# Batch normalization over 512 MiB on one core: one DMA ring in groups of three, or a load ring and a store ring with hand-placed semaphores

## The chip, the cores and the metric

The kernel runs on one core of one Trainium2 chip. The metric is the device time of one execution in microseconds (us). The kernel before was run nine times: its median is 2487.23 us, with the runs between 2486.8 and 2489.03 us.

## The reference

The reference is batch normalization in its inference form, on a float32 tensor of 32 x 256 x 128 x 128. Each of the 256 channels has its own four numbers (gamma, beta, running mean and running variance), so that the whole computation is one multiplication and one addition for each element:

```python
def reference(x, gamma, beta, running_mean, running_var):
    eps = 1e-5
    ...
    return gamma * (x - mean) / np.sqrt(var + eps) + beta
```

The input has 536.87 MB and the output has as much. Every byte is read once and written once.

## The kernel before

**Tiles.** The 256 channels are two blocks of 128, one channel in each of the 128 partitions of the on-chip memory. With 32 images this makes 64 tiles. A tile has 128 partitions x 16384 float32 elements, which is 8.389 MB; each partition's row of 64 KiB is contiguous in device memory, and so is the whole tile. There are three buffers (NBUF = 3) of that size, and a tile is changed in place.

**Parameters.** At the start ScalarE's queue issues four loads of 1 KB, one for each parameter vector (line 58). VectorE transposes them (line 66) and copies them into place (line 71), ScalarE takes the square root (line 78), and four short VectorE instructions (lines 85 to 88) make a scale and a shift for each channel.

**The main loop.** Tile i goes through three steps: load(i) (line 51) is one DMA from device memory into a buffer, compute(i) (line 93) is one VectorE instruction that multiplies by the scale and adds the shift, and store(i) (line 104) is one DMA from the buffer to device memory. Loads and stores are all issued by SyncE (SP in the profile), and so lie in one ring, which the profile calls q1. The order is written out by hand: GROUPS lists twenty groups of three tiles and two of two, and AHEAD is 0. For each group the kernel issues the computes, then the group's stores, then the loads of the next group. On SP's ring this gives three loads, three stores, three loads, three stores, and so on. The pool of three buffers puts in the waits: a load waits until the store that last used its buffer has landed, and a store waits for its compute. Such a wait stands on SP, and everything issued later by SP stands behind it. Where an instruction has to wait for more than one semaphore, a separate semaphore instruction of 17 ns is put ahead of it (42 ahead of stores, 22 ahead of loads).

Of the kernel before, what the change touches and what calls it, by code (L numbers as in the profile page):

```python
# [1 line left out]

# [4 lines left out]


NBUF = 3
GROUPS = [3] * 20 + [2, 2]  # L10

AHEAD = 0


@with_exitstack
def kernel(
    ctx: ExitStack,
    tc: tile.TileContext,
    x: bass.AP,
    gamma: bass.AP,  # L20
    beta: bass.AP,
    running_mean: bass.AP,
    running_var: bass.AP,
    out: bass.AP,
):
    nc = tc.nc
    eps = 1e-5
    f32 = mybir.dt.float32

    N, C, H, W = x.shape  # L30
    P = nc.NUM_PARTITIONS
    assert C % P == 0
    NCB = C // P
    HW = H * W
    NT = N * NCB
    B = 32
    NQ = P // B
    assert sum(GROUPS) == NT and max(GROUPS) <= NBUF

    params = ctx.enter_context(tc.tile_pool(name="params", bufs=1))  # L40
    data = ctx.enter_context(tc.tile_pool(name="data", bufs=NBUF))

    xr = x.rearrange("n (cb p) h w -> (n cb) p (h w)", p=P)
    outr = out.rearrange("n (cb p) h w -> (n cb) p (h w)", p=P)

    ctx.enter_context(tc.manual_schedule())
    tiles = {}

    def load(i):
        t = data.tile([P, HW], f32, tag="t")  # L50
        nc.sync.dma_start(out=t[:], in_=xr[i])  # L51
        tiles[i] = t


    rows = params.tile([B, C], f32, tag="rows")
    nc.vector.memset(rows, 0.0)  # L56
    for r, ap in enumerate((running_var, gamma, beta, running_mean)):
        nc.scalar.dma_start(out=rows[r : r + 1, :], in_=ap.rearrange("(o c) -> o c", o=1))

    for i in range(AHEAD + GROUPS[0]):  # L60
        load(i)

    eps_t = params.tile([P, 1], f32, tag="eps")
    nc.vector.memset(eps_t, eps)  # L64
    turned = params.tile([B, C], f32, tag="turned")
    nc.vector.transpose(out=turned[:], in_=rows[:])  # L66

    par = params.tile([P, NCB, 4], f32, tag="par")
    blocks = turned.rearrange("p (cb q r) -> p cb q r", cb=NCB, q=NQ)
    for q in range(NQ):  # L70
        nc.vector.tensor_copy(out=par[q * B : (q + 1) * B], in_=blocks[:, :, q, 0:4])  # L71
    var_t, gamma_t, beta_t, mean_t = (par[:, :, r] for r in range(4))

    scale_t = params.tile([P, NCB], f32, tag="scale")
    shift_t = params.tile([P, NCB], f32, tag="shift")
    tmp_t = params.tile([P, NCB], f32, tag="tmp")

    nc.scalar.activation(  # L78
        out=tmp_t[:],
        in_=var_t,  # L80
        func=mybir.ActivationFunctionType.Sqrt,
        bias=eps_t[:],
        scale=1.0,
    )
    nc.vector.reciprocal(out=tmp_t[:], in_=tmp_t[:])  # L85
    nc.vector.tensor_mul(out=scale_t[:], in0=gamma_t, in1=tmp_t[:])  # L86
    nc.vector.tensor_mul(out=tmp_t[:], in0=mean_t, in1=scale_t[:])  # L87
    nc.vector.tensor_sub(out=shift_t[:], in0=beta_t, in1=tmp_t[:])  # L88

    def compute(i):  # L90
        t = tiles[i]
        cb = i % NCB
        nc.vector.tensor_scalar(  # L93
            out=t[:],
            in0=t[:],
            scalar1=scale_t[:, cb : cb + 1],
            scalar2=shift_t[:, cb : cb + 1],
            op0=mybir.AluOpType.mult,
            op1=mybir.AluOpType.add,
        )  # L100

    def store(i):
        t = tiles.pop(i)
        nc.sync.dma_start(out=outr[i], in_=t[:])  # L104


    first = 0
    for g, size in enumerate(GROUPS):
        idxs = range(first, first + size)
        for i in idxs:  # L110
            compute(i)
        for i in idxs:
            store(i)
        first += size
        more = GROUPS[g + 1] if g + 1 < len(GROUPS) else 0
        for i in range(first + AHEAD, min(first + AHEAD + more, NT)):
            load(i)


# [1 line left out]
_INS = ['x', 'gamma', 'beta', 'running_mean', 'running_var']  # L121
_OUTS = [((32, 256, 128, 128), 'float32')]


# [23 lines left out]
```

## Time and profile before

| | before |
|---|---|
| median of nine runs | 2487.23 us |
| the profiled execution, its whole time | 2488.09 us |
| span of the profiled execution | 2486.3 us |
| VectorE busy | 566.0 us (23% of the span) |
| ScalarE busy | 1.6 us |
| bytes moved by DMA | 1073.77 MB, a mean of 432 GB/s |
| one VectorE instruction on a tile | 8812 ns |
| one load, from issue to landing (median) | 58.0 us |
| one store, from issue to landing (median) | 49.1 us |

The profile's page gives the busy time of the engines, then the span in 40 equal slices with the busy share of the 16 DMA engines and the rate that they reached, then the DMA queues, the chain of work that ended last, and the groups of instructions. Line numbers such as L93 are lines of the kernel. A trailing q (SPq, ACTq) means an engine's queue of instructions, where DMAs are issued and where waits stand. The timeline lists instructions by their start. The "us to landing" of a DMA counts from its issue, so it holds the time in which the DMA stood behind others in its ring.

### The profile page before, as it was taken

The page shows a single profiled execution, that of the slowest core. Times are in us where ns is not written, and L with a number is a line of the kernel's source. Part 1 is how long each engine was busy: PE and PEld are TensorE (multiplying, and loading weights), DVE is VectorE, ACT ScalarE, POOL GpSimd, SP SyncE. Part 2 cuts the span into 40 slices and gives each one's busy share as a digit, 9 for nine tenths or more (in the row PEclk, how much of TensorE's full clock was granted, in tenths as well). Part 3 has the DMA queues.
Part 4 walks back from the last instruction along what each step waited for, and adds up shares of the span by engine and source line. Part 5 has one row for each costly group of instructions (what it writes and reads, how often), then busy time and mean ns, then how long its engine had stood idle before and what let it go on. Part 6 is the DMA issues. An engine that isn't in the chain of part 4 may idle for free.

```text
span 2486.3 us, 383 instructions
## 1 busy us (share of the span) xinstructions
DVE 566.0 (23%) x75; ACT 1.6 (0%) x2; POOL 0.2 (0%) x4
## 2 busy tenths in 40 slices
DVE  3140404121222212140404121221213040403112
ACT  0000000000000000000000000000000000000000
POOL 0000000000000000000000000000000000000000
DMA  9999999999999999999999999999999999999998
GB/s 422 423 438 439 423 438 437 434 427 438 433 428 438 435 431 433 433 437 430 433 438 435 427 437 437 431 431 438 437 427 435 434 435 430 433 437 434 431 435 384
DMA packets 18442, 1073.77 MB, mean 432 GB/s; under 512 B 2052, under 2 KB 2056, under 8 KB 2056
## 3 DMA queue, kind: packets, MB, share of 16 engines
q1 hardware_dynamic: 18432, 1073.75, 99.9%
q14 instruction: 2, 0.02, 0.0%
q10 hardware_dynamic: 8, 0.00, 0.0%
HBM read 536.88 MB, written 536.87 MB: 432 GB/s over the span
## 4 chain that ended last, share of the span: by engine, by line
another core or an unknown queue 73%; DVE 22%; DMA 4%; issue 0%; DVEq 0%; SPq 0%
DVE t L93 22%; DMA t<-in_x_dram 4%; DVEq L93 0%; SPq L51 0%; SPq L104 0%
## 5 line engine op out<-in xcount | busy, mean ns | idle before, releaser
L93 DVE TENSOR_SCALAR t<-t,scale_t,shift_t 128x16384 f32<-128x16384 f32 x64 | 564.0, 8812 | 1866.8 <-DMA t<-in_x_dram 1866.8
L66 DVE STREAM_TRANSPOSE turned<-rows 32x256 f32<-32x256 f32 x1 | 0.4, 433 | 21.3 <-DMA rows<-in_running_mean_dram 21.3
L78 ACT ACT_TABLE_LOAD x1 | 1.3, 1283 | 2.6 <-issue 2.6
L71 DVE COPY par<-turned 32x8 f32<-32x8 f32 x4 | 0.6, 162 | 0.1
L56 DVE MEMSET rows<- 32x256 f32 x1 | 0.3, 272 | 0.8 <-PEq L132 0.8
L78 ACT ACTIVATE tmp_t<-par,eps_t 128x2 f32<-128x2 f32 x1 | 0.3, 297 | 19.7 <-DVE par L71 19.7
L85 DVE RECIPROCAL tmp_t<-tmp_t 128x2 f32<-128x2 f32 x1 | 0.2, 166 | 0.4 <-ACT tmp_t L78 0.4
L87 DVE TENSOR_TENSOR tmp_t<-par,scale_t 128x2 f32<-128x2 f32 x1 | 0.2, 163 | 0.0
L86 DVE TENSOR_TENSOR scale_t<-par,tmp_t 128x2 f32<-128x2 f32 x1 | 0.2, 161 | 0.0
L88 DVE TENSOR_TENSOR shift_t<-par,tmp_t 128x2 f32<-128x2 f32 x1 | 0.2, 160 | 0.0
L132 POOL MEMSET const-uint8-127<- 128x1 uint8 x1 | 0.1, 102 | 0.0
L132 POOL MEMSET const-bfloat16-1.0<- 128x1 bf16 x1 | 0.1, 101 | 0.0
L132 POOL MEMSET const-float32-0.0<- 128x1 f32 x1 | 0.1, 98 | 0.2 <-issue 0.2
L132 POOL MEMSET const-float32-1.0<- 128x1 f32 x1 | 0.1, 98 | 0.0
L64 DVE MEMSET eps_t<- 128x1 f32 x1 | 0.1, 59 | 0.0
## 6 DMA issues: line engine op xcount, KB each, us to landing
t<-in_x_dram SPq DMA_DIRECT2D x64, 58.0
out_dram<-t SPq DMA_DIRECT2D x64, 49.1
rows<-in_running_var_dram ACTq DMA_DIRECT2D x1, 1.0 KB
rows<-in_gamma_dram ACTq DMA_DIRECT2D x1, 1.0 KB
rows<-in_beta_dram ACTq DMA_DIRECT2D x1, 1.0 KB
rows<-in_running_mean_dram ACTq DMA_DIRECT2D x1, 1.0 KB
```

The lines of the kernel that those rows point to most:

```text
L56: nc.vector.memset(rows, 0.0)
L64: nc.vector.memset(eps_t, eps)
L66: nc.vector.transpose(out=turned[:], in_=rows[:])
L71: nc.vector.tensor_copy(out=par[q * B : (q + 1) * B], in_=blocks[:, :, q, 0:4])
L78: nc.scalar.activation(out=tmp_t[:], in_=var_t, func=mybir.ActivationFunctionType.Sqrt, bias=eps_t[:], scale=1.0,)
L85: nc.vector.reciprocal(out=tmp_t[:], in_=tmp_t[:])
L86: nc.vector.tensor_mul(out=scale_t[:], in0=gamma_t, in1=tmp_t[:])
L87: nc.vector.tensor_mul(out=tmp_t[:], in0=mean_t, in1=scale_t[:])
L88: nc.vector.tensor_sub(out=shift_t[:], in0=beta_t, in1=tmp_t[:])
L93: nc.vector.tensor_scalar(out=t[:], in0=t[:], scalar1=scale_t[:, cb : cb + 1], scalar2=shift_t[:, cb : cb + 1], op0=mybir.AluOpType.mult, ...
L132: nc = _bacc.Bacc("TRN2", target_bir_lowering=False, num_devices=1)
```

## The change

The changed kernel has the same tiles, the same number of buffers and the same three steps for each tile. What differs:

- All 64 loads are issued by SyncE, one after another (line 76 of the changed kernel). All 64 stores are issued by ScalarE's queue (line 124), on the ring that also carries the four parameter loads. There are no groups.
- The three buffers are fixed slots; tile i uses slot i modulo 3. Waits are placed by hand and each instruction has one: a load waits until the slot's previous store has landed (stored[s]), a compute waits for its load (loaded[s]), and a store waits for its compute (done). The pool's waits and the separate semaphore instructions ahead of DMAs are gone; the first compute alone has a second wait ahead of it.
- In the preparation of the parameters each VectorE instruction waits for the one before it by a semaphore (vec), and the two temporary tiles that were written twice are now separate tiles. The memset of eps comes ahead of that of rows.
- The whole body stands in one critical section, which adds a branch and a no-operation at its start and end.

```diff
-GROUPS = [3] * 20 + [2, 2]
-
-AHEAD = 0
...
-    def load(i):
-        t = data.tile([P, HW], f32, tag="t")
-        nc.sync.dma_start(out=t[:], in_=xr[i])
-        tiles[i] = t
...
+    data = ctx.enter_context(tc.tile_pool(name="data", bufs=1))
+    bufs = [data.tile([P, HW], f32, name=f"t{s}", tag=f"t{s}") for s in range(NBUF)]
...
+        def step(inst, sem=None, value=None):
+
+            if sem is not None:
+                inst._wait_ge(sem, value)
+            elif count[0]:
+                inst._wait_ge(vec, count[0])
+            inst.then_inc(vec, 1)
+            count[0] += 1
+            return count[0]
...
+        def load(i):
+            s, turn = i % NBUF, i // NBUF
+            inst = nc.sync.dma_start(out=bufs[s][:], in_=xr[i])
+            if turn:
+                inst._wait_ge(stored[s], 16 * turn)
+            inst.then_inc(loaded[s], 16)
...
+        for i in range(NT):
+            load(i)
...
-    def store(i):
-        t = tiles.pop(i)
-        nc.sync.dma_start(out=outr[i], in_=t[:])
...
-    first = 0
-    for g, size in enumerate(GROUPS):
-        idxs = range(first, first + size)
-        for i in idxs:
-            compute(i)
-        for i in idxs:
-            store(i)
-        first += size
-        more = GROUPS[g + 1] if g + 1 < len(GROUPS) else 0
-        for i in range(first + AHEAD, min(first + AHEAD + more, NT)):
-            load(i)
...
+        for i in range(NT):
+            s, turn, cb = i % NBUF, i // NBUF, i % NCB
+            nc.vector.tensor_scalar(
+                out=bufs[s][:],
+                in0=bufs[s][:],
...
+            )._wait_ge(loaded[s], 16 * (turn + 1)).then_inc(done, 1)
+
+        for i in range(NT):
+            s = i % NBUF
+            nc.scalar.dma_start(out=outr[i], in_=bufs[s][:])._wait_ge(done, i + 1).then_inc(stored[s], 16)
+
+        for s in range(NBUF):
+            nc.sync.wait_ge(stored[s], 16 * ((NT - s + NBUF - 1) // NBUF))
```

More of the change, by code (lines that the diff above doesn't have):

```diff
@@ L37 @@
     NQ = P // B
-    assert sum(GROUPS) == NT and max(GROUPS) <= NBUF
-    params = ctx.enter_context(tc.tile_pool(name="params", bufs=1))
-    data = ctx.enter_context(tc.tile_pool(name="data", bufs=NBUF))
     xr = x.rearrange("n (cb p) h w -> (n cb) p (h w)", p=P)
     outr = out.rearrange("n (cb p) h w -> (n cb) p (h w)", p=P)
-    ctx.enter_context(tc.manual_schedule())
-    tiles = {}
-    def load(i):
-        t = data.tile([P, HW], f32, tag="t")
-        nc.sync.dma_start(out=t[:], in_=xr[i])
-        tiles[i] = t
@@ L55 @@
[L55 to L60, printed above, removed]
-        load(i)
[L63 to L100, printed above, removed]
@@ L102, in store @@
-    def store(i):
-        t = tiles.pop(i)
-        nc.sync.dma_start(out=outr[i], in_=t[:])
-    first = 0
-    for g, size in enumerate(GROUPS):
-        idxs = range(first, first + size)
-        for i in idxs:
-            compute(i)
-        for i in idxs:
-            store(i)
-        first += size
-        more = GROUPS[g + 1] if g + 1 < len(GROUPS) else 0
-        for i in range(first + AHEAD, min(first + AHEAD + more, NT)):
-            load(i)
+    params = ctx.enter_context(tc.tile_pool(name="params", bufs=1))
@@ new lines @@
+    data = ctx.enter_context(tc.tile_pool(name="data", bufs=1))
+    bufs = [data.tile([P, HW], f32, name=f"t{s}", tag=f"t{s}") for s in range(NBUF)]
+    rows = params.tile([B, C], f32, name="rows", tag="rows")
+    turned = params.tile([B, C], f32, name="turned", tag="turned")
+    par = params.tile([P, NCB, 4], f32, name="par", tag="par")
+    eps_t = params.tile([P, 1], f32, name="eps_t", tag="eps")
+    std_t = params.tile([P, NCB], f32, name="std_t", tag="std")
+    rstd_t = params.tile([P, NCB], f32, name="rstd_t", tag="rstd")
@@ new lines @@
+    scale_t = params.tile([P, NCB], f32, name="scale_t", tag="scale")
+    ms_t = params.tile([P, NCB], f32, name="ms_t", tag="ms")
+    shift_t = params.tile([P, NCB], f32, name="shift_t", tag="shift")
+    loaded = [tc.alloc_semaphore(f"loaded{s}") for s in range(NBUF)]
+    stored = [tc.alloc_semaphore(f"stored{s}") for s in range(NBUF)]
+    done = tc.alloc_semaphore("done")
+    fetched = tc.alloc_semaphore("fetched")
+    vec = tc.alloc_semaphore("vec")
+    act = tc.alloc_semaphore("act")
@@ new lines @@
+    with tc.tile_critical():
+        count = [0]
+        def step(inst, sem=None, value=None):
[13 more added lines that the diff above has]
+        for i in range(NT):
+            load(i)
+        step(nc.vector.memset(eps_t[:], eps))
+        zeroed = step(nc.vector.memset(rows[:], 0.0))
+        for r, ap in enumerate((running_var, gamma, beta, running_mean)):
+            inst = nc.scalar.dma_start(out=rows[r : r + 1, :], in_=ap.rearrange("(o c) -> o c", o=1))
+            if r == 0:
+                inst._wait_ge(vec, zeroed)
+            inst.then_inc(fetched, 16)
+        step(nc.vector.transpose(out=turned[:], in_=rows[:]), fetched, 64)
+        blocks = turned.rearrange("p (cb q r) -> p cb q r", cb=NCB, q=NQ)
+        for q in range(NQ):
+            placed = step(nc.vector.tensor_copy(out=par[q * B : (q + 1) * B], in_=blocks[:, :, q, 0:4]))
+        var_t, gamma_t, beta_t, mean_t = (par[:, :, r] for r in range(4))
+        nc.scalar.activation(
+            out=std_t[:],
+            in_=var_t,
+            func=mybir.ActivationFunctionType.Sqrt,
+            bias=eps_t[:],
+            scale=1.0,
+        )._wait_ge(vec, placed).then_inc(act, 1)
+        step(nc.vector.reciprocal(out=rstd_t[:], in_=std_t[:]), act, 1)
+        step(nc.vector.tensor_mul(out=scale_t[:], in0=gamma_t, in1=rstd_t[:]))
+        step(nc.vector.tensor_mul(out=ms_t[:], in0=mean_t, in1=scale_t[:]))
+        ready = step(nc.vector.tensor_sub(out=shift_t[:], in0=beta_t, in1=ms_t[:]))
+        nc.vector.wait_ge(vec, ready)
+        for i in range(NT):
[3 more added lines that the diff above has]
+                in0=bufs[s][:],
+                scalar1=scale_t[:, cb : cb + 1],
+                scalar2=shift_t[:, cb : cb + 1],
+                op0=mybir.AluOpType.mult,
+                op1=mybir.AluOpType.add,
+            )._wait_ge(loaded[s], 16 * (turn + 1)).then_inc(done, 1)
[4 more added lines that the diff above has]
+            nc.sync.wait_ge(stored[s], 16 * ((NT - s + NBUF - 1) // NBUF))
```

## The prediction

> **What bounds the kernel now.** I read the page's slices first, then the queues, then the groups, and then the timeline. The slices and the queue table:
>
> ```profile
> span 2486.3 us, 383 instructions
> DVE  3140404121222212140404121221213040403112
> DMA  9999999999999999999999999999999999999998
> GB/s 422 423 438 439 423 438 437 434 427 438 433 428 438 435 431 433 433 437 430 433 438 435 427 437 437 431 431 438 437 427 435 434 435 430 433 437 434 431 435 384
> q1 hardware_dynamic: 18432, 1073.75, 99.9%
> ```
>
> See that the DMA engines are busy in every slice, while VectorE has three idle tenths in four. The one ring q1 takes 99.9% of the engines' time, so there is no idle DMA time to be won in the body. The groups and the DMA issues:
>
> ```profile
> L93 DVE TENSOR_SCALAR t<-t,scale_t,shift_t 128x16384 f32<-128x16384 f32 x64 | 564.0, 8812 | 1866.8 <-DMA t<-in_x_dram 1866.8
> L66 DVE STREAM_TRANSPOSE turned<-rows 32x256 f32<-32x256 f32 x1 | 0.4, 433 | 21.3 <-DMA rows<-in_running_mean_dram 21.3
> t<-in_x_dram SPq DMA_DIRECT2D x64, 58.0
> out_dram<-t SPq DMA_DIRECT2D x64, 49.1
> ```
>
> VectorE's idle time ends with a load every time. How the ring alternates is seen in the timeline of one group:
>
> ```profile
> 139.84 8.81 DVE L93 TENSOR_SCALAR t<-t,scale_t,shift_t 128x16384 f32<-128x16384 f32 x1 [68.63 <-DMA t<-in_x_dram]
> 148.68 39.20 SPq L104 DMA_DIRECT2D out_dram<-t  x3
> 159.24 8.81 DVE L93 TENSOR_SCALAR t<-t,scale_t,shift_t 128x16384 f32<-128x16384 f32 x1 [10.59 <-DMA t<-in_x_dram]
> 178.71 8.81 DVE L93 TENSOR_SCALAR t<-t,scale_t,shift_t 128x16384 f32<-128x16384 f32 x1 [10.65 <-DMA t<-in_x_dram]
> 197.94 39.35 SPq L51 DMA_DIRECT2D t<-in_x_dram  x3
> 256.29 8.81 DVE L93 TENSOR_SCALAR t<-t,scale_t,shift_t 128x16384 f32<-128x16384 f32 x1 [68.77 <-DMA t<-in_x_dram]
> ```
>
> Loads of a group land 19.40 and 19.47 us apart (159.24 - 139.84, 178.71 - 159.24); the first load of the next group lands 77.58 us later, with three stores ahead of it. The group takes 116.45 us. Over 19 groups, from the compute at 139.84 to that at 2349.57, a group takes 2209.73 / 19 = 116.30 us, and a transfer 116.30 / 6 = 19.384 us. That times 128 is 2481.2 us; the 5 us missing to the span are the start (first issue at 0.73), landing times and the end. The path that sets the end is 128 transfers one after another. Reads and writes of the big tensor go in turns: three tiles in, three tiles out.
>
> [...] q10, the ring of the parameter loads, has 8 packets. Packets of q1 are one row of 64 KiB, 19.384 / 8 = 2.42 us each, as an engine moves 8 rows of a tile. If each of the 8 waits for one of those, the four loads land after 8 x 2.42 = 19.4 us and a landing; VectorE waited 21.3 us for them. [...] The trace shows an issue at some 0.34 us beside 19.4 us of transfer, hidden. [...] This trace moves 8.3886 MB / 19.384 = 432.8 GB/s, with one direction at a time; it doesn't show the two together.
>
> **The change part by part.**
>
> *Order and rings.* A load and a store are now in flight together, and an engine takes their packets in turn. Let a transfer be 19.4 us alone and 38.8 us at half rate. Load 0 lands near 22; its compute starts at 24.7 as before (the parameters), and store 0 is issued at 33.5. Load 1 then has 1.2 + 38.8 - 33.5 = 6.5 us left and takes 13; store 0 has 12.9 us left and takes another 25.8, beside load 2. From there it repeats: a load ends 13 us after a store, a store 25.8 us after a load, one tile every 38.8 us. Does an engine run dry? A slot needs 38.8 for the load, 8.8 for the compute, 38.8 for the store and two landings of at most 1.84 us (load 1 landed 40.55 us after its first packet at 1.16, and 2 x 19.384 = 38.77 of that is transfer), 90.1 us in all, of 3 x 38.8 = 116.4 us. Only one slot at a time is in compute or landing, and the other two hold DMAs. So the engines stay busy, and by count alone the time is unchanged: 0 us.
>
> *The turns between rings.* Per tile an engine moves 8 + 8 packets in turn, 64 x 16 = 1024 changes of direction where there were 43. One ns each is 1 us of the end, and 5 us (0.2%) is about what a measurement of this kernel can tell from no change. The trace has no such traffic, so I bound its price. From above: load 0 landed 21.7 us after its issue and load 1 within 1.84 us of its transfer time, though 16 changes to and from q10 had passed on an engine; 1.84 / 16 = 0.115 us, times 1024 is 118 us. From the single ring: within a group loads come 19.46 us apart (mean of 42 in the timeline), across groups 77.33 (mean of 20), so a store with its share of two changes takes (77.33 - 19.46) / 3 = 19.29 us. [...]
>
> *Waits.* The 64 semaphore instructions of 17 ns on SP (1.1 us in all) go, at no gain: each lies under a queued transfer. A load's wait on the slot's store holds up later loads on SP; of these the next is blocked by a later store anyway. A store's wait for its compute now stands on ScalarE, which has nothing else once the square root is done. Ahead of SP's loads no store stands any more; what is late next is the same transfer time. VectorE's waits in the preparation (nine instructions, below 0.1 us each as the rows of 0.16 us follow each other in 0.2) put the first compute some 0.5 us later; loads 1 and 2, which run to 59, cover it. Without that cover it would cost its 0.5 us. Cost 0.
>
> *Start and end.* A branch and a no-operation ahead of the first load: 0 to 0.5 us, from the 0.73 at which it was issued; I take 0.3. At the end, when load 63 has moved, store 62 has 12.9 us left, at full rate now; the landing and compute of tile 63 take 1.84 + 8.81 = 10.65 us and are covered by 2 us. If the cover were gone, at most 10.65 us would lie open. Cost 0.
>
> *Sum.* 27.6 + 0.3 = 27.9 us on the profiled execution: 2488.09 + 27.9 = 2516.0. That execution is 0.86 us above the median, so 2487.2 + 27.9 = 2515 us for the median.
>
> **The rivals.** *No change* (2488): the engines pass from ring to ring without loss[...] and the total stays 128 x 19.384. For it: full DMA slices before and after, the same bytes. [...] *Faster* (2474): [...] For it: two rings always have a packet ready. Against it: the one ring had its next DMA queued too[...]. *Much slower* (2605): a change costs the upper bound of 0.115 us, or memory does badly at mixed reads and writes; 2487 + 118. For it: nothing in the trace has tested mixed traffic at length. Against it: the bound lumps the whole landing time into the changes. *The rings don't overlap*: then order and time stay as before, within "no change".
>
> **How the numbers follow.** [...] 0.46, 2515 us, own range 2495 to 2560. Much slower: 0.10. No change: 0.26. Faster: 0.18. So slower by over 0.2% is 0.56, within 0.2% 0.26, faster 0.18. The range runs from the faster case, 2474, to the upper bound, 2605. The cases are of both signs, and the likeliest one's own range stands above.
>
> **What would show it.** Right: store landings near 38.8 to 57 us with loads near 51, computes evenly spaced at about 39.2 us (2 x 19.6) in place of 19.4, 19.5, 77.3; DMA slices full[...]. No change shows 38.8 us, faster 38.6, much slower 40.6. If slices fall below 9, or if the end shows an open compute of 8.8 us, my claim that no engine runs dry is wrong. If computes come in bunches, the rings do not share by turns.

## The result and the profile after

The changed kernel takes 2504.02 us (median of 9 runs, 2501.75 to 2509.16). The kernel before, measured beside it, takes 2487.3 us. The ratio is 1.0068, with a 95% interval of 1.0059 to 1.0076: slower by 0.68%, or 16.7 us. The profiled execution took 2505.35 us with a span of 2503.6 us, 17.3 us over the span before.

From the page of the changed kernel, its span, slices and queues:

```profile
span 2503.6 us, 263 instructions
DVE  3122221222212122121221222212212122121221
DMA  9999999999999999999999999999999999999996
GB/s 418 435 433 427 433 431 435 433 435 436 435 435 435 436 433 423 432 433 435 435 435 427 435 432 431 436 435 436 427 427 424 433 435 435 431 429 436 431 433 301
q1 hardware_dynamic: 9216, 536.88, 49.9%
q10 hardware_dynamic: 9224, 536.88, 49.5%
```

The bytes now lie half on each ring, and the slices of the body show the same rates as before. The last slice stands out: 301 GB/s, where it was 384, and a 6 in the busy share. The groups and issues of the same page:

```profile
L113 DVE TENSOR_SCALAR t<-t,scale_t,shift_t 128x16384 f32<-128x16384 f32 x64 | 564.0, 8812 | 1888.3 <-DMA t<-in_x_dram 1888.2
t<-in_x_dram SPq DMA_DIRECT2D x64, 48.6
out_dram<-t ACTq DMA_DIRECT2D x64, 59.3
```

VectorE's work is the same to the nanosecond; it waits 21.4 us longer for loads. Where the time is lost is seen by stretches. The columns are the stretch, its length, the busy time of VectorE, ScalarE and GpSimd, the clock, the busy share of the DMA engines, and their GB/s. First the kernel before:

```profile
100.00:2400.00 2300.00, 519.89 (x59) 0.00 (x0) 0.00 (x0) 1.00 1.00 434
...
2478.00:2484.00 6.00, 0.00 (x0) 0.00 (x0) 0.00 (x0) 1.00 0.28 120
2484.00:2486.30 2.30, 0.00 (x0) 0.00 (x0) 0.00 (x0) 1.00 0.00 0
```

Then the changed kernel:

```profile
100.00:2400.00 2300.00, 519.91 (x59) 0.00 (x0) 0.00 (x0) 1.00 1.00 433
...
2464.00:2478.00 14.00, 8.81 (x1) 0.00 (x0) 0.00 (x0) 1.00 0.09 37
2478.00:2490.00 12.00, 0.00 (x0) 0.00 (x0) 0.00 (x0) 1.00 1.01 437
2490.00:2496.00 6.00, 0.00 (x0) 0.00 (x0) 0.00 (x0) 1.00 1.19 513
2496.00:2500.00 4.00, 0.00 (x0) 0.00 (x0) 0.00 (x0) 1.00 0.08 33
2500.00:2503.60 3.60, 0.00 (x0) 0.00 (x0) 0.00 (x0) 1.00 0.00 0
```

(A packet is counted where it starts, so a stretch can show a share over 1.) In the body, loads and stores together move 433 GB/s, as against 434 with one direction at a time. Over 2300 us that difference is 2300 x 1 / 434 = 5 us (the rates are rounded, so this is rough; the bytes in the packet records give 4.5). From 2464 to 2478 the DMA engines are 9% busy. One engine of 16 is 6%, and one engine moves 65,536 bytes in 2.42 us, 27 GB/s: one engine is at work and fifteen have nothing to do (by the packet records they end between 2464 and 2468). The tail from 2464 on moves 14 x 37 + 12 x 437 + 6 x 513 + 4 x 33 thousand bytes, 8.97 MB, for which 433 GB/s would need 20.7 us. It takes 39.6 us, so 18.9 are lost. The same sum for the kernel before, from 2478 on, is 0.72 MB, 1.7 us at its rate, in 8.3 us: 6.6 lost. The tail thus costs some 12.3 us more and the body some 5, which together are the 17.3 us between the two spans.

What SyncE waited for from 2380 on in the changed kernel (engine and line, what released it, total, times, longest):

```profile
SPq L76 <- DMA out_dram<-t: 76.7, 2, 38.5
SPq L127 <- DMA out_dram<-t: 62.7, 1, 62.7
SPq L61 <- DMA out_dram<-t: 19.2, 1, 19.2
```

The last load is issued at 2420.0 and SP then waits 62.7 us, to 2483, and 19.2 us, to 2502. Those are the landings of stores 62 and 63, one whole transfer apart. A transfer has landed when the last of its engines has finished. So for the last engine store 63, issued at 2477.4, followed on store 62 with no gap; the other fifteen had been done with store 62 for 10 us and more.

The trace's record of semaphore increments has 16 for each DMA of a tile, one for each engine (in the packet records, a 4-byte packet after an engine's eight rows). From it I worked out how far the last engine is behind. In the changed kernel, in means over stretches of 250 us, the last increment comes 1.7, 4.7, 7.2, 11.7 and 19.9 us after the second last, and then the means stay between 17 and 20 us until the last store. In the kernel before it is never more than 0.7 us behind the second last, and 6 us behind the median engine at the end.

Following the last engine's packets from landing to landing shows where it loses time between 200 and 1060 us: in load packets, most often the first of a tile, which takes 0.1 to 1.1 us over the usual 2.418. There are 32 that run over by more than 0.1 us, 14 us in all; the other fifteen engines have 29 between them. 14 us is about the time for which the other engines stand idle at the end (10 to 14.5 us); why the landings lie still further apart, some 24 us, the packets' lengths don't explain. After about 1100 us the long packets come on all engines: from 1100 to 2400 us the trace has 249, 95 us or 6 us an engine, and the last engine has its share and no more. In the same stretch the kernel before has 44, 23 us in all. So the lag stops growing there, and the 5 us of the body are not the lag of one engine but longer load packets on all. Neither was in my prediction.

### The profile page after: what moved, and what is told of

Read it like the earlier page. It is cut to its first block, busy times and chain, and to the rows that moved or that the text cites. A ratio compares the mean times of both kernels' runs of the same rounds, so it can differ in the third digit from the quotient of the medians.

```text
span 2503.6 us, 263 instructions
## 1 busy us (share of the span) xinstructions
DVE 566.0 (23%) x75; ACT 1.6 (0%) x2; POOL 0.2 (0%) x4
## 4 chain that ended last, share of the span: by engine, by line
another core or an unknown queue 93%; DMA 4%; DVE 1%; SPq 1%; issue 0%; ACTq 0%; ACT 0%; DVEq 0%
DMA t<-in_x_dram 2%; DMA out_dram<-t 2%; DMA rows<-in_running_mean_dram 1%; SPq L76 1%; DVE t L113 1%; ACTq L88 0%; DVE par L96 0%; DVE turned L92 0%; ACT std_t L98 0%; DVE rows L86 0%; DVE rstd_t L105 0%; DVE shift_t L108 0%; DVE ms_t L107 0%; DVE scale_t L106 0%
## 6 DMA issues: line engine op xcount, KB each, us to landing
t<-in_x_dram SPq DMA_DIRECT2D x64, 48.6
out_dram<-t ACTq DMA_DIRECT2D x64, 59.3
```

## The experiments

Two theories stood after the result. **Turns** is that of the prediction: each change between the rings has a price, now 16.7 / 1024 = 16 ns. **Lag**: turns are free, but one engine falls behind, the end waits for it, and something about whole tiles on two rings lets that happen. A third, **waits**, blames the hand-placed semaphores.

### Which part of the change: the ring or the waits

*one_ring_sems* keeps the semaphores and puts the stores back on SyncE, in the order of before:

```diff
-            nc.scalar.dma_start(out=outr[i], in_=bufs[s][:])._wait_ge(done, i + 1).then_inc(stored[s], 16)
+            nc.sync.dma_start(out=outr[i], in_=bufs[s][:])._wait_ge(done, i + 1).then_inc(stored[s], 16)
...
+        groups = [3] * 20 + [2, 2]
```

> The changed kernel with its hand-placed semaphores, but all stores issued by SyncE in the order of the kernel before (three stores, three loads). If the second ring is what costs the 16.7 us (by the turns between rings, or by one DMA engine that falls behind when loads and stores lie in different rings): about 2487 us. If the hand-placed waits cost it: about 2504 us.

Measured: 2487.17 us, 1.0002 of before (0.9994 to 1.0011).

*pool_two_rings* is the kernel before with one word changed:

```diff
-        nc.sync.dma_start(out=outr[i], in_=t[:])
+        nc.scalar.dma_start(out=outr[i], in_=t[:])
```

> The kernel before with one word changed: stores issued by ScalarE. If the second ring costs the time: about 2504 us, computes spaced evenly near 39 us. If the hand-placed waits cost it: about 2487 us.

Measured: 2504.05 us, 1.0072 (1.006 to 1.0085). The four corners of this square settle it: the second ring costs the time, and the waits cost nothing that can be measured. The last engine is 25.1 us behind the median one (mean of the landings from 1250 to 2400 us, as for every lag below), as in the changed kernel (24.3); in *one_ring_sems* it is 4.1.

### Do turns have a price

*split4_two_rings* cuts each transfer into four column pieces, and *split4_one_ring* does the same to *one_ring_sems*. The edit to the load (the store's is alike):

```diff
+            for k in range(PARTS):
+                f = slice(k * W4, (k + 1) * W4)
+                inst = nc.sync.dma_start(out=bufs[s][:, f], in_=xr[i][:, f])
```

> The changed kernel with each load and each store cut into four DMAs of 4096 columns, so that packets are 16 KiB and an engine changes direction 4096 times in place of 1024. If each change has a price (16.7 us / 1024 = 16 ns): 3072 more changes, 50 us over what the cut itself costs on one ring, so 67 us over the one-ring kernel with the same cut. If one engine falls behind for a reason that doesn't go with the number of changes: about 17 us over that kernel.

> The control for the cut: one ring, order of the kernel before, each load and store in four DMAs of 4096 columns. It shows what smaller packets cost without turns between rings: between 2487 us (nothing) and 2560 us [...].

Measured: 2499.87 us (1.0053, 1.004 to 1.0065) on two rings and 2507.15 us (1.0082, 1.0068 to 1.0095) on one. With many more turns, two rings are 7 us faster than the control, not 67 slower as **turns** has it. Turns at a price are out. Nor are they 17 us slower, as the other expectation had it: that took the lag to stay, and the cut removes it. The cut has a price of its own: a packet of 16 KiB takes 611 ns, four of them 2.444 us in place of 2.418. On two rings the last engine is 2.2 us behind the median.

How often an engine really turns can be counted in the packet records, since its next packet starts within 4 ns of the end of the one before. In the changed kernel 53% of the packets are followed by one of the other ring, which makes some 545 turns an engine in place of the 1024 that I had counted; in *split4_two_rings* there are some 3650, in the cut into two below some 1810.

*split2_two_rings* and *split2_one_ring* are the same kernels with PARTS = 2.

> The changed kernel with each load and store cut into two DMAs of 8192 columns: packets of 32 KiB, 2048 changes of direction. The cut into four took 2499.9 us on two rings and 2507.2 on one, so the cut itself costs about 20 us there, or a third of it here (one more packet a row in place of three): 7 us. If packets smaller than 64 KiB alone take away the lag of one engine: 2487 + 7 - 2 = about 2492 us. If the lag shrinks with the packet: half of 16.7 us stays, about 2502 us. If changes had a price: above 2511 us.

> The control for the cut into two: one ring, order of the kernel before, two DMAs of 8192 columns for each load and store. The cut into four cost 20 us on one ring, for three more packets a row; one more packet a row: 2487 + 7 = 2494 us. Beside it the two-ring kernel with the same cut took 2487.05 us. If the control is at 2487 too, packets of 32 KiB are free and turns between rings are as well.

Measured: 2487.05 us (1.0001, 0.9992 to 1.0009; all twelve runs within 0.11 us) on two rings, and 2495.48 us (1.0033, 1.0022 to 1.0045) on one. The first is 5 us below the 2492 expected without lag, since on two rings the cut does not cost what it costs on one. The body of *split2_two_rings* and its last slices:

```profile
100.00:2400.00 2300.00, 519.91 (x59) 0.00 (x0) 0.00 (x0) 1.00 1.00 433
...
2470.00:2480.00 10.00, 0.00 (x0) 0.00 (x0) 0.00 (x0) 1.00 1.00 433
2480.00:2485.20 5.20, 0.00 (x0) 0.00 (x0) 0.00 (x0) 1.00 0.28 120
```

The rate of the body is that of the changed kernel, 433, and the tail with one engine at work is gone: fifteen engines no longer stand idle ahead of the last store. The last engine is 1.6 us behind the median. Both kernels have two rings and mix directions throughout; without the lag the loss is gone. Together with the sum of the tail above, this ties the loss to the lag. The cut removes the long load packets too (3 that run over by more than 0.1 us from 200 to 2400 us), so it doesn't tell the one from the other.

### What puts one engine behind

*params_first* issues the parameter loads on SyncE, ahead of the tiles:

```diff
-        for i in range(NT):
-            load(i)
...
-            inst = nc.scalar.dma_start(out=rows[r : r + 1, :], in_=ap.rearrange("(o c) -> o c", o=1))
+            inst = nc.sync.dma_start(out=rows[r : r + 1, :], in_=ap.rearrange("(o c) -> o c", o=1))
...
+        for i in range(NT):
+            load(i)
```

> The changed kernel with the four parameter loads issued by SyncE ahead of the first tile, so that they take no turns beside tile loads. If the engine that falls behind (the trace of the changed kernel shows one alone, about 2 us behind the next after four tiles and 17 to 20 us behind it from the middle of the run) is put behind by the parameters' packets and then kept there: near 2489 us. If not: 2504 us.

Measured: 2504.29 us (1.0066, 1.0045 to 1.0087), lag 25.0 us. The four runs lie between 2495.4 and 2507.89. The parameters are not the seed.

*shifted_reads* reads other tiles than it writes (in_=xr[(i + 21) % NT] in the load):

```diff
-            inst = nc.sync.dma_start(out=bufs[s][:], in_=xr[i])
+            inst = nc.sync.dma_start(out=bufs[s][:], in_=xr[(i + 21) % NT])
```

> The changed kernel, but tile i is read from the place of tile (i + 21) modulo 64 of x, so that the addresses of reads and writes under way together stand in another relation (the output then holds other tiles than the reference). If the relation of addresses makes one engine's reads slow: a time other than 2504 us by more than 4 us, most likely near 2489. If addresses don't matter: 2504 us.

Measured: 2503.49 us (1.007, 1.0053 to 1.0087), lag 24.6 us. This other relation of addresses changes nothing; others were not tried.

*rows4_two_rings* cuts by partitions, four DMAs of 32 partitions each:

```diff
+                f = slice(k * R4, (k + 1) * R4)
+                inst = nc.sync.dma_start(out=bufs[s][f, :], in_=xr[i][f, :])
```

> The changed kernel with each load and store cut into four DMAs of 32 partitions: four times the DMAs, but packets of 64 KiB as in the changed kernel, and 1024 changes of direction. If packets of 64 KiB in turn on two rings make one engine fall behind: about 2504 us. If it is the size of the DMA [...]: near 2489 us. A fixed price for a change of direction would also give 2504 us.

Measured: 3704.57 us (1.4706, 1.4613 to 1.48), far from both expectations. Packets got slower themselves, as the page of its profiled execution shows (the slowest of the four, 3746.35 us):

```profile
DMA packets 24589, 1073.82 MB, mean 287 GB/s; under 512 B 8196, under 2 KB 8200, under 8 KB 8200
q1 hardware_dynamic: 12288, 536.89, 62.9%
q10 hardware_dynamic: 12296, 536.89, 36.9%
```

Loads take 63% of the engines' time for half of the bytes; a load packet takes 4.59 us in the mean, 1.9 times the usual 2.418, a store packet 2.69, 1.1 times. The run therefore says nothing on the lag; its design put in another cost. Why the packets of these DMAs of 32 partitions last longer, those of loads above all, was not shown.

*loads_cut* and *stores_cut* cut one direction alone into two pieces. The edit of *loads_cut* (that of *stores_cut* does the same to the store):

```diff
-            inst = nc.sync.dma_start(out=bufs[s][:], in_=xr[i])
...
+            for k in range(PARTS):
+                f = slice(k * W4, (k + 1) * W4)
+                inst = nc.sync.dma_start(out=bufs[s][:, f], in_=xr[i][:, f])
```

> The changed kernel with only the loads cut into two DMAs of 8192 columns (packets of 32 KiB); stores stay whole. With both cut the time was 2487.05 us and one engine no longer fell far behind. If long load packets of 64 KiB are what holds the last engine up: no lag, 2482 to 2488 us. If the store packets of 64 KiB between them hold it up: about 2504 us.

> The changed kernel with only the stores cut into two DMAs of 8192 columns; loads stay whole. The counterpart: if the load packets of 64 KiB are the cause, the lag stays and the time is 2504 to 2510 us; if the store packets are, 2482 to 2488 us.

Measured: loads cut, 2636.05 us (1.06, 1.0582 to 1.0617); stores cut, 2486.77 us (0.9999, 0.9991 to 1.0008). Both expectations failed for *loads_cut*. Of the body of *loads_cut*:

```profile
100.00:2500.00 2400.00, 519.93 (x59) 0.00 (x0) 0.00 (x0) 1.00 0.99 409
```

and of *stores_cut*:

```profile
100.00:2400.00 2300.00, 519.92 (x59) 0.00 (x0) 0.00 (x0) 1.00 1.00 433
...
2480.00:2485.00 5.00, 0.00 (x0) 0.00 (x0) 0.00 (x0) 1.00 0.31 131
```

With the loads cut the engines are busy (0.99) and still move 409 GB/s only: the packets last longer, a mean of 1263 ns for a load's 32 KiB and 2539 ns for a store's 64 KiB. The medians are the usual 1213 and 2418; some packets, 11% of the loads' and 21% of the stores', are over 5% longer. The last engine is 16.8 us behind the median in the mean of all landings, but 3 us in the stores' alone, and the second last is with it (1.1 us between them), so more than one engine is late, and with loads. (The halves of a load share a semaphore, so these figures are rough.) With the stores cut no engine is (1.7 us), though load packets are of 64 KiB. So long load packets by themselves are not the cause. What differs is the share of each ring: if turns go by packets, the ring with the smaller packets gets less while both have work. At the start of the kernel before they did: q10's eight packets began 2.42 to 2.46 us apart, one packet of q1 (2.418 us) between each two. The landings agree with the shares. With the stores cut a load lands in 33.3 us and a half of a store in 57.8; with the loads cut a half of a load lands in 58.8 us and a store in 37.7 (medians from issue; *stores_cut* first):

```profile
out_dram<-t ACTq DMA_DIRECT2D x128, 4096.0 KB, 57.8
t<-in_x_dram SPq DMA_DIRECT2D x64, 33.3
...
t<-in_x_dram SPq DMA_DIRECT2D x128, 4096.0 KB, 58.8
out_dram<-t ACTq DMA_DIRECT2D x64, 37.7
```

That the share is what removes or makes the lag is argued from these two runs, not shown by itself.

*tiny_compute* cuts VectorE's instruction to 64 columns; the other columns are stored as they were loaded:

```diff
-                out=bufs[s][:],
-                in0=bufs[s][:],
+                out=bufs[s][:, 0:64],
+                in0=bufs[s][:, 0:64],
```

> The changed kernel with VectorE's instruction cut to 64 of 16384 columns (the other columns are stored as they were loaded). In the trace the last engine's first load packet after a landing runs long while VectorE works on the tile that has just landed. If VectorE's access to the on-chip memory is what stretches it: near 2487 us. If not: about 2504 us.

Measured: a median of 2488.71 us (1.001, 0.9996 to 1.0024), but twenty runs spread from 2480.82 to 2505.23. Neither theory has that. In the profiled execution, one of the longer ones with a span of 2498.4 us, the last engine is within 5.5 us of the first to 1500 us, and in the last loads it is 26 us behind. So engines can fall behind while VectorE is idle 99% of the time, and VectorE's long access to the buffer is not needed for it. Here the second last engine is only some 3.4 us ahead of the last, so it is not one engine alone. The edit changes two things, VectorE's access and the time between a landing and its store, which is 8.8 us shorter. One of them makes the lag less likely; which one isn't shown.

## Why the prediction was right and where it was wrong

**The direction and the range were right**: slower, 2504 us within 2495 to 2560 of the likeliest case. The size was too large, 27.9 us for 16.7, and the mechanism under it was wrong. That the direction came out right was therefore luck: it rested on a price for turns that the runs don't show.

**The step that failed is "The turns between rings"**, where I put 27.6 us on 1024 changes, 27 ns each. No trace had shown such a price. The body runs at 433 GB/s with both directions in flight, 434 before; 27.6 us spread over the run would have taken 1.1% off that rate (27.6 / 2487), to some 429. The count was too high as well, 545 turns for 1024. Two rings with some 1810 and 3650 turns are 8.4 and 7.3 us *faster* than their controls on one ring. The price is zero within what these runs can tell, or below it. What stood in its place is the lag of one engine, some 12.3 us in the tail, and longer load packets on all engines, some 5 us in the body.

**The step "Start and end"** was half right. For the last engine the cover at the end held: its store 62 lasted until store 63 was there. For the other fifteen it didn't. They were idle for 10 to 14.5 us by the DMA records, the landing and compute of 10.65 us and more. I walked the rings forward as if sixteen engines were one. A compute waits for its load on the last engine too (that of tile 63 began at 2468.55, 0.02 us after the landing), so each engine ahead of it gives its lead back at the end. The sign that I had named for this, an open compute at the end, is there: VectorE's 8.81 us lie in the stretch in which the engines are 9% busy.

**"Order and rings"** was right for the body: the count of 0 us for order, load landings near 51 us (48.6), store landings near 57 (59.3). From the third on the computes came 39.28 us apart to 1188 us and 38.80 from there to 2430 (39.02 over all), where I had 39.2. That near hit was for the wrong reason. A price on every turn would stay to the end, but it is the engine's growing lag that stretches the first part, and once the lag has settled, most intervals are 38.6.

**"Waits"**: 0, as forecast (*one_ring_sems*). The first compute began at 25.21 in place of 24.72, 0.49 us later, for 0.5 forecast; the first load was issued at 0.95 in place of 0.73, for 0.3 forecast.

**The rivals.** "No change" had the right argument, that turns are free, and the wrong time, because it too treated the engines alike. "Faster" is not seen against the kernel before, only between kernels with the same cut (8.4 and 7.3 us). "Much slower" was off for this kernel, but its second half, memory that does badly at mixed traffic, has a counterpart in *loads_cut*: there packets last 4 to 5% longer in the mean, at 2636 us. Whether memory is the cause was not shown.

**What stays open.** It is shown that the second ring causes the loss, that some 12 of the 17 us take the form of one engine's lag, and that cutting the stores, or both directions, removes the loss. Why one engine's load packets run long in the first 1000 us, why its lag settles near 25 us, and why the share of the rings matters so much were not settled. Nor do the records name the engine, so I can't say whether it is the same one in each run. It is not one chip's fault: *pool_two_rings* ran on another chip than *params_first* and *shifted_reads*, and all three have the lag.

No version beat both kernels: *stores_cut*, at 2486.77, lies within the noise of before.

## What to carry to other kernels

Here the DMA engines were full (a busy share of 1.00 in the body), a second ring brought no bandwidth (433 GB/s for 434), and most of its cost did not show in the body's rate. In such a case look at the last slices and at the spread of one transfer's sixteen increments. The end waited for the slowest engine, so hold two numbers, the mean rate and the last engine's lead or lag. If two rings are wanted, try smaller pieces on both, or on the ring whose transfers may wait (here the stores): halves took 2487.05 us on both and 2486.77 on the stores alone. On the loads alone they cost 6% here.

## What the runs showed of the hardware that was not expected

- Rows of 64 KiB moved as one packet each of 2.418 us (median) in either direction; 32 KiB took 1.213 us and 16 KiB 0.611 us, so cutting a row in four cost 26 ns.
- A completion increment (a packet of 4 bytes, 9 ns) takes a turn of its ring: in the last engine's packets of the changed kernel, two store packets follow each other where a load's increment lies between them. On all engines, with each packet put behind the one that ended where it starts, some 1000 of the 1024 increments of loads lie between two store packets.
- With two rings an engine turned after 53% of its packets in the changed kernel and after 88 to 89% in the kernels with both directions cut.
- Pieces of 128 x 8192 for the loads beside whole stores cost 6%, the mirror image nothing.
- DMAs of 32 partitions moved 287 GB/s, with the same 64 KiB rows.
